# Four places instead of two for the output-gate tiles of the mLSTM in a hybrid block

## The chip, the cores and the metric

The kernel runs on one core of a Trainium2 chip. The core has five engines that run side by side, each through its own queue of instructions in order: PE (TensorE) for matmuls and transposes, DVE (VectorE), ACT (ScalarE) and POOL (GpSimd) for the work on elements, and SP (SyncE), which here issues nearly all DMAs. Data lies in DRAM, in the on-chip memory (SBUF, 128 partitions) and in PSUM, into which PE writes.

The metric is the time of one execution on the device in microseconds. Times inside an execution are counted from its first instruction. A trace is of one execution, recorded by the hardware profiler.

## The reference: what is computed

The input x is [1, 1024, 1024]. One layer projects its norm h with a wide matrix and runs two branches:

```python
qk = silu(conv(a_q, a_k));  mq, mk, mv = heads(...)          # 4 heads of width 256
h_fw = mlstm_one_direction(mq, mk, mv, i_fw, lf_fw)
h_bw = flip(mlstm_one_direction(flip(mq), flip(mk), flip(mv), flip(i_bw), flip(lf_bw)))
hm  = rmsnorm(h_fw + h_bw, ml_norm_g)
y_a = hm * sigmoid(a_o) * silu(a_z)                          # the output gate
y_b = rmsnorm(diff_attention(dq, dk, da_v, lam)) * silu(b_z) # 8 heads of width 128
mix = sigmoid(g_a + gb[0]) * (y_a @ w_branch_a) + sigmoid(g_b + gb[1]) * (y_b @ w_branch_b)
out = rmsnorm(x + mix @ w_out, final_g)
```

The change concerns the line of `y_a`. The product of the two functions of a_o and a_z is made early in the kernel and kept in DRAM; it is called the gate here.

## The kernel before, in words

**Precision.** Every float32 matrix product is made of three products of halves: a high part (names ending in H, cast by ACT) and a low part (names ending in L, a subtraction on DVE or POOL).

**Stages.** The kernel runs one stage after the other: the norm and the transposition of x; the products for a_k, a_q, a_o and a_z with the convolution, whose results go to DRAM (the gate to the eight tensors `gm`, 128 channels by 1024 positions each); the attention, head by head, whose results go to the eight tensors `yb`; the mLSTM (from about 1107 us to about 1398 us in the trace), whose results go to the eight tensors `ya`; and the output stage, which first multiplies `yb` with `w_branch_b`, then `ya` with `w_branch_a`, and then the mix with `w_out`. Products for the two mixing gates (`gate_units`: 48 matmuls into a PSUM tile `pj` per half, a tanh on ACT at L837 into a tile `gt`, a store at L838 into `tga` or `tgb`) are spread over all stages as filling for PE.

**The mLSTM.** Both directions of a head are computed together. Its 1024 positions are four chunks of 256, and each chunk is two steps of 128 positions, so a head has eight steps (t = 0 to 7 in `ml_units`, L1239). In a step PE makes the state's products (`I`), the product of the weights with the values (`P`), the scores of the next step (`S`) and transposes of the weights W (`T`); DVE turns the scores into W (L1139), the denominators into factors (L1165 to L1176), combines the two directions in W (L1185) and adds up the result `hm` (L1188, L1209); POOL masks W (L1136); ACT scales (L1179, L1183) and casts (L1198). A head's tail (norm, transposition, gate) runs during the first steps of the next head: the scaling by the norm (L1216) at t = 1 and 2, the output `O(0)` for the first 512 positions at t = 2 and `O(1)` for the other 512 at t = 3. The last head's tail is the list `late` (L1307), put ahead of the filling that follows.

**The gate tiles.** `load_g(half)` (L1218) loads two tiles `gA` of 128 channels by 512 positions (i = 0, 1) for one half of a head's positions. `out(i, half)` (L1223) transposes `hm` on PE into a PSUM tile `T`, multiplies it with the norm's gain and the gate tile on DVE (L1228), with the result in the same gate tile, and stores this tile to `ya` (L1229). In the written program `load_g(0)` of a head stands at t = 0 of the next head and `load_g(1)` at t = 2, behind `O(0)` (L1300); for the last head, `load_g(0)` stands at L1306 and `load_g(1)` behind `O(0)` in `late`. A head needs four gate tiles, and the tag `gA` has two places in SBUF.

**What sets the order.** PE's instructions run in the order in which the program writes them (`keep(E.PE)`, L1522). The order of all other queues is set at build by a planner: among the instructions that can go, it takes the one that is earliest in the program, and it counts a tile as free to be written once its place has no user left. A load can therefore go out long before its place in the program, but not before a place of its tag is free. On the chip each instruction waits for the semaphores of what it needs, and what stands behind it in its queue waits too.

**The pools.** SBUF is handed out in pools, one per stage: `w1` for the attention, `w2` for the mLSTM, `wy` and `wr` for the output stage. They use the same bytes one after the other (`reuse_waits="tile"`: a tile waits for the last user of its own bytes). `gA` is the last tag of `w2`. `w2` closes behind `late` and the filling beside it (L1574), then `wy` opens.

**The output stage's start.** `load_y` (L1310) loads one of the eight `yb` tensors into a tile `yraw` (L1312; two places), casts it on ACT into a tile `sl_yb` (L1314) and subtracts on DVE into another (L1315). The first matmul group of the stage goes through all eight in turn, with three matmuls each (L429). On ACT, L1314 stands among the tanh of the filling (L837) and the casts of the next weights (L204, into one of three places `wH`).

Of the kernel before, what the change touches and what calls it, by code (L numbers as in the profile page):

```python
# [7 lines left out]
F32 = mybir.dt.float32  # L8
# [101 lines left out]
class Block:  # L110
# [917 lines left out]
    def ml_head(self, n, st):  # L1028


        v, a, p, q, w2 = self.v, self.a, self.p, self.q, self.w2
# [185 lines left out]

        def load_g(half):  # L1218
            for i in range(2):
                st["g", i] = w2.tile([128, 512], F32, name="gA", tag="gA", bufs=2)  # L1220
                q.dma_start(out=st["g", i], in_=self.gd_ml[2 * n + i][:, half * 512:(half + 1) * 512])

        def out(i, half):  # L1223
            ps = self.bank("T")
            for k in range(4):
# [8 lines left out]
                    v=self.v_units("av", n, vv, order=(3, 2, 1, 0)), weigh=step(weigh),  # L1234
                    state=lambda c, d: [do(state, c, d, i) for i in range(2)], split=step(split), S=step(scores),
                    I=step(t_tile), T=step(transposes), P=step(pv), scale=step(scale), g=step(load_g),
                    O=lambda half: [do(out, i, half) for i in range(2)])

# [402 lines left out]
```

## Time and profile before

| What | Value |
|---|---|
| Median of 3 runs | 1697.88 us (1696.63 to 1701.5) |
| The profiled execution's own time | 1699.79 us |
| Its span, first to last instruction | 1698.0 us |
| Mean granted TensorE clock | 0.996 |
| Busy share of PE / DVE / ACT / POOL | 97% / 59% / 45% / 37% |
| Gate loads gA<-gm (L1221) | 16 of 256 KB, first at 1150.2 us, last at 1393.5 us |
| Multiplies with the gate (L1228) | 16 of 128x512, median 750 ns, first at 1224.0 us, last at 1397.0 us |
| Stores ya<-gA (L1229) | 16, first at 1224.7 us, last at 1397.8 us |

How to read the rows that follow. A row of a timeline has its start, its length, engine and line, operation, the tile written and the tiles read, their shapes, and in brackets the idle time of the engine just before it and what ended it. Engine names with a q (SPq) are instructions of the queue itself, such as the issue of a DMA; "x2" joins two in a row. A row of windows has a stretch's start and end, its length, the busy time and the count of instructions of PE, PE's weight loads, DVE, ACT and POOL, the granted clock of PE (1.00 is full speed), the share of the DMA engines' time and GB/s. Matmuls overlap, so the length of one is more than the time between two.

### The profile page before, as it was taken

Reading aid. Unit: us, or ns where it says so; the run is one execution under the profiler, and the core shown is the slowest. Engines: PE = TensorE matmul, PEld = TensorE weight load, DVE = VectorE, ACT = ScalarE, POOL = GpSimd, SP = SyncE. Lnnn points to the kernel's source line nnn. Section 1 sums busy time; section 2 is a strip of 40 time slices with the busy share of each in tenths; the row PEclk is TensorE's granted clock in tenths of the full one; section 3 lists DMA queues with packets and bytes.
Section 4 is the critical chain, followed back from the end, with each engine's and each line's share of the span. In section 5 each row is a group of like instructions: output and inputs, shape, how many; then the busy total and the mean of one; then the engine's idle time right before and its main releaser. Section 6 shows DMA issues by size and latency. Waiting matters only on the chain. (4 is left out here: it accounts for less than half of the span.)

```text
span 1698.0 us, 25367 instructions
## 1 busy us (share of the span) xinstructions
PE 1650.1 (97%) x9431; PEld 1387.7 (82%) x9431; DVE 994.1 (59%) x1799; ACT 760.0 (45%) x1522; POOL 635.3 (37%) x712
## 2 busy tenths in 40 slices
PE   7999999999999999999999999999999898999998
PEld 5777887887888988898888888889999777888887
DVE  5778668674277666766666765126666644135533
ACT  6454555543254454454445454325656644022221
POOL 5767676665343235424351431221331311212000
PEclk9999999999999999999999999999999999999999
DMA  5334434434231213221230221175554327344222
GB/s 179 101 118 134 137 115 134 124 124 137 75 81 44 63 38 87 63 63 37 76 88 26 63 75 63 50 208 155 143 170 140 104 93 244 119 142 136 87 92 83
DMA packets 175630, 178.79 MB, mean 105 GB/s; under 512 B 12185, under 2 KB 135410, under 8 KB 175506
## 3 DMA queue, kind: packets, MB, share of 16 engines
q1 hardware_dynamic: 174594, 175.58, 34.5%
q8 instruction: 74, 1.21, 0.3%
q10 hardware_dynamic: 912, 1.59, 0.2%
q14 instruction: 50, 0.41, 0.1%
HBM read 114.11 MB, written 46.24 MB: 94 GB/s over the span
## 5 line engine op out<-in xcount | busy, mean ns | idle before, releaser
L429 PE MATMUL pj<-hH,wH 128*128 128x512 f32 x640 | 266.3, 416 | 3.3 <-ACT f L542 1.5
L429 PE MATMUL pj<-hH,wL 128*128 128x512 f32 x640 | 251.9, 394 | 1.7 <-POOL wL L207 1.7
L429 PE MATMUL pj<-hL,wH 128*128 128x512 f32 x640 | 250.6, 392 | 0.2 <-DVE hL L580 0.2
L209 POOL TENSOR_TENSOR wL<-raw,wH 128x1024 fp32r<-128x1024 f32 x41 | 99.6, 2429 | 284.2 <-ACT wH L204 281.8
L928 ACT ACTIVATE e<-S,nm 128x1024 f32<-128x1024 f32 x128 | 142.7, 1115 | 134.2 <-DVE nm L926 133.9
L948 DVE TENSOR_TENSOR pL<-T,pH 128x512 fp32r<-128x512 f32 x128 | 87.9, 688 | 117.4 <-ACT pH L947 116.7
L926 DVE TENSOR_REDUCE nm<-S 128x1 f32<-128x1024 f32 x128 | 150.5, 1217 | 10.1 <-PE S L923 9.3
L429 PEld LDWEIGHTS pj<-hH,wH 128*128 128x128 f32 x640 | 120.7, 189 | 37.8 <-issue 14.4
L451 PE MATMUL pj<-wH,hH 128*128 128x256 f32 x512 | 149.9, 293 | 1.6 <-DVE vL L1035 1.3
L451 PE MATMUL pj<-wL,hH 128*128 128x256 f32 x512 | 144.9, 283 | 1.4 <-POOL wL L207 1.4
L429 PEld LDWEIGHTS pj<-hH,wL 128*128 128x128 f32 x640 | 120.4, 188 | 30.1 <-POOL wL L207 3.1
L451 PE MATMUL pj<-wH,hL 128*128 128x256 f32 x512 | 144.5, 282 | 0.0
L429 PEld LDWEIGHTS pj<-hL,wH 128*128 128x128 f32 x640 | 121.0, 189 | 18.2 <-DVE hL L580 0.6
L429 PE MATMUL pj<-sl_yb,wH 128*128 128x512 f32 x384 | 121.8, 397 | 4.7 <-ACT sl_yb L1314 2.1
L947 ACT CAST pH<-T 128x512 fp32r<-128x512 f32 x128 | 74.7, 584 | 100.5 <-PE T L131 99.9
L204 ACT CAST wH<-raw 128x1024 fp32r<-128x1024 f32 x56 | 58.8, 1050 | 126.8 <-PE pj L429 86.4
L923 PE MATMUL S<-kst,qq 64*128 64x512 f32 x768 | 106.5, 408 | 0.0
L451 PEld LDWEIGHTS pj<-wH,hH 128*128 128x128 f32 x512 | 97.7, 191 | 6.8 <-issue 3.9
L451 PEld LDWEIGHTS pj<-wL,hH 128*128 128x128 f32 x512 | 97.5, 190 | 2.3 <-POOL wL L207 2.3
L451 PEld LDWEIGHTS pj<-wH,hL 128*128 128x128 f32 x512 | 97.7, 191 | 0.1
L429 PEld LDWEIGHTS pj<-sl_yb,wH 128*128 128x128 f32 x384 | 73.3, 191 | 22.8 <-DVE sl_yb L1315 3.3
L934 DVE SCALAR_TENSOR_TENSOR e<-e,r,e 128x1024 f32<-128x1024 f32 x64 | 88.8, 1388 | 2.2
(358 smaller groups left out, 4099.9 us busy)
## 6 DMA issues: line engine op xcount, KB each, us to landing
raw<-in_w_in_dram SPq DMA_DIRECT2D x88, 512.0 KB, 3.8
kst<-hl SPq DMA_DIRECT2D x64, 128.0 KB, 2.4
qq<-hl SPq DMA_DIRECT2D x64, 128.0 KB, 2.4
x<-in_x_dram SPq DMA_DIRECT2D x8, 512.0 KB, 6.2
cak<-y SPq DMA_DIRECT2D x16, 256.0 KB, 2.3
cakH<-cin SPq DMA_DIRECT2D x16, 256.0 KB, 4.4
cakL<-tz SPq DMA_DIRECT2D x16, 256.0 KB, 4.0
gm<-oz SPq DMA_DIRECT2D x16, 256.0 KB, 2.8
```

What stands on the lines that cost most here:

```text
L204: self.a.copy(wH, raw)
L209: self.p.tensor_tensor(out=wL, in0=raw, in1=wHf, op=ALU.subtract)
L429: self.t.matmul(ps, lhsT=l[:, k, :], rhs=r, start=(n == 0), stop=(n == 23))
L451: self.t.matmul(ps[:, i, :], lhsT=l, rhs=r[:, k, :], start=(kh == 0 and k == 0 and m == 0), stop=(kh == 1 and k == 3 and m == 2))
L923: self.t.matmul(ps[:, o], lhsT=qq[r, x, c], rhs=k[r, y, o], start=(m == 0), stop=(m == 2))
L926: v.tensor_reduce(out=nm, in_=ps, axis=AX.X, op=ALU.max, negate=True)
L928: a.activation(out=e, in_=ps, func=AF.Exp, bias=nm[:, 0:1], accum_out=Z[:, j, t:t + 1])
L934: v.scalar_tensor_tensor(out=e0, in0=e, scalar=r[:, 0:1], in1=e0, op0=ALU.mult, op1=ALU.add)
L947: a.copy(pH[:, :, s], ps)
L948: v.tensor_tensor(out=pL[:, :, s], in0=ps, in1=pH[:, :, s].bitcast(F32), op=ALU.subtract)
```

## The change

The tag of the gate tiles gets four places in SBUF instead of two. Nothing else in the program is touched: the instructions, their number and PE's order are the same. Two more tiles of 2 KB a partition make the pool `w2` 4 KB larger; since the pool ends at a fixed address and `gA` is its last tag, the other tiles of the pool lie 4 KB lower.

```diff
         def load_g(half):
             for i in range(2):
-                st["g", i] = w2.tile([128, 512], F32, name="gA", tag="gA", bufs=2)
+                st["g", i] = w2.tile([128, 512], F32, name="gA", tag="gA", bufs=4)
                 q.dma_start(out=st["g", i], in_=self.gd_ml[2 * n + i][:, half * 512:(half + 1) * 512])
```

## The prediction

> **What bounds the kernel now.** I read the page first: TensorE is busy nearly all the time, so a change counts only where it shortens a wait of PE or a slow stretch of its clock.
>
> ```profile
> PE 1650.1 (97%) x9431; PEld 1387.7 (82%) x9431; DVE 994.1 (59%) x1799; ACT 760.0 (45%) x1522; POOL 635.3 (37%) x712
> ```
>
> Next I asked for the two lines that use the gate tiles (gA): their loads (L1221) and their multiplies (L1228), with what DVE waited for ahead of a multiply.
>
> ```profile
> L1221 SPq DMA_DIRECT2D gA<-gm x16: 319/320/531, 1150.2 to 1393.5; - x16
> DMA to landing us min/median/max: 3.1/3.9/5.2
> ...
> L1228 DVE SCALAR_TENSOR_TENSOR gA<-T,mlg,gA x16: 741/750/753, 1224.0 to 1397.0; 128x512 f32<-128x512 f32 x16
>   DMA gA<-gm: 7.0, 3
>   issue: 2.2, 1
> ```
>
> DVE waits for a gate tile ahead of four of the 16 multiplies: three are put down to the DMA, and the one put down to "issue" is of the same cause, as the timeline below shows. PE does not wait for a gate tile by name. The windows show where it stands (length, then PE busy; the number behind POOL is the granted clock):
>
> ```profile
> 1160.00:1200.00 40.00, 39.98 (x336) 39.70 (x335) 26.19 (x101) 22.63 (x56) 6.16 (x21) 1.00 0.40 108
> ...
> 1352.80:1357.40 4.60, 0.69 (x3) 0.14 (x1) 2.44 (x11) 0.88 (x2) 0.00 (x0) 0.99 0.39 116
> 1357.40:1360.80 3.40, 3.33 (x10) 2.76 (x11) 0.83 (x3) 1.17 (x3) 0.69 (x2) 0.51 0.61 189
> 1420.00:1430.70 10.70, 6.46 (x23) 4.12 (x23) 4.90 (x4) 5.54 (x7) 2.49 (x1) 0.92 0.78 225
> 1430.70:1435.80 5.10, 5.10 (x12) 4.05 (x13) 1.95 (x3) 2.09 (x2) 0.00 (x0) 0.50 0.54 169
> 1435.80:1512.00 76.20, 76.20 (x337) 63.07 (x337) 14.90 (x18) 10.81 (x11) 16.73 (x7) 1.00 0.39 124
> ```
>
> There are two holes, from 1353 and from 1420, and behind each a stretch at half clock. Behind the second PE is full for 76 us: what is gained ahead of it is kept.
>
> **Place A: the second half of head 2, during head 3.** The timelines of DVE, PE and SP:
>
> ```profile
> 1352.74 0.75 DVE L1228 SCALAR_TENSOR_TENSOR gA<-T,mlg,gA 128x512 f32<-128x512 f32 x1 [0.71 <-DMA gA<-gm]
> 1354.09 0.15 DVE L1176 TENSOR_TENSOR al<-rr,gc_sint 128x2 f32<-128x2 f32 x1
> 1356.40 0.75 DVE L1228 SCALAR_TENSOR_TENSOR gA<-T,mlg,gA 128x512 f32<-128x512 f32 x1 [2.15 <-issue]
> 1357.07 0.34 DVE L1185 SCALAR_TENSOR_TENSOR W<-W,rr,W 128x128 f32<-128x128 f32 x1
> ...
> 1354.44 0.33 PE L131 MATMUL T<-ident,W 128*128 128x128 f32 x1 [1.28 <-ACT W L1183]
> 1357.47 0.48 PE L131 MATMUL T<-ident,W 128*128 128x128 f32 x1 [2.70 <-DVE W L1185]
> ...
> 1348.74 0.38 SPq L1229 DMA_DIRECT2D ya<-gA  x1
> 1353.34 0.32 SPq L1221 DMA_DIRECT2D gA<-gm  x1
> ```
>
> With two places, a half's load can start only when the store of the half before has left the same place. SP holds the load until 1353.34, 4.6 us behind the store of 1348.74. It lands near 1356.4 (the shortest landing above, 3.1 us), and that is when the multiply starts. PE waits for the next head's W, which stands behind the multiply in DVE's queue. With four places this load needs no store of its own head: it goes out one half earlier. The store and the reload around 1353 stay, and so does SP's wait there, but the reload then carries head 3's first half, which is first used at 1388.53 (below).
>
> The sum for A: without the 0.71 and the 2.15, `al` ends at 1353.53 (1354.24 - 0.71), the multiply takes 0.67 of DVE's queue (1357.07 - 1356.40), and L1185 ends at 1354.54 (another 0.34) instead of 1357.41. PE resumes 2.9 us earlier. Of its waits 1.28 - 0.71 = 0.6 stays and about as much for L1185: the chain from rr by L1183 to L1185 is late next, not the load. Waits that short leave the clock alone; even one of 1.80 did, as the window behind it shows:
>
> ```profile
> 1333.18 0.44 PE L131 MATMUL T<-ident,W 128*128 128x128 f32 x2 [1.80 <-DVE W L1185]
> ...
> 1333.20:1340.00 6.80, 6.80 (x47) 6.17 (x48) 5.45 (x21) 6.48 (x18) 1.39 (x4) 1.00 0.12 36
> ```
>
> So the 3.3 us of busy PE at 0.51 shrink by half, 1.6 us. A gives 2.9 + 1.6 = 4.5 us; at the least 0 (the loads stay where they are), at the most 1.28 + 2.70 + 1.6 = 5.6.
>
> In sentences that the rest can do without: the Trainium skill (TensorE: Matmul & The Clock Gate, Part 1) says that the clock gate looks at free-running windows of some 3.4 us and passes half of the pulses behind an idle one, which gives an estimate of 1.7 us lost by one window. The trace's 3.40 us at 0.51 agree.
>
> **Heads 0 and 1** give nothing: the four waits for gA are the two of A and the two of B, and no other multiply waits.
>
> **Place B: the end of head 3 and the start of the output stage.**
>
> ```profile
> 1389.43 1.23 PE T L131 x8
> ...
> 1388.53 1.41 DVE L1228 SCALAR_TENSOR_TENSOR gA<-T,mlg,gA 128x512 f32<-128x512 f32 x2 [2.16 <-PE T L131]
> 1395.77 0.75 DVE L1228 SCALAR_TENSOR_TENSOR gA<-T,mlg,gA 128x512 f32<-128x512 f32 x1 [5.82 <-DMA gA<-gm]
> 1397.02 0.75 DVE L1228 SCALAR_TENSOR_TENSOR gA<-T,mlg,gA 128x512 f32<-128x512 f32 x1 [0.51 <-DMA gA<-gm]
> 1429.37 1.22 DVE L1315 TENSOR_TENSOR sl_yb<-yraw,sl_yb 128x1024 fp32r<-128x1024 f32 x1 [1.90 <-ACT sl_yb L1314]
> ...
> 1392.90 0.96 SPq L1221 DMA_DIRECT2D gA<-gm  x2
> 1393.96 0.38 SPq L838 DMA_DIRECT2D tga<-gt  x1
> 1396.54 1.58 SPq L1229 DMA_DIRECT2D ya<-gA  x2
> 1398.23 0.37 SPq L1312 DMA_DIRECT2D yraw<-yb  x1
> ...
> 1408.87 1.05 ACT L204 CAST wH<-raw 128x1024 fp32r<-128x1024 f32 x1 [2.95 <-PE pj L429]
> 1419.21 1.05 ACT L1314 CAST sl_yb<-yraw 128x1024 fp32r<-128x1024 f32 x1 [6.03 <-DMA yraw<-yb]
> ...
> 1419.55 0.39 PE L429 MATMUL pj<-hH,wL 128*128 128x512 f32 x1
> 1421.46 0.40 PE L429 MATMUL pj<-sl_yb,wL 128*128 128x512 f32 x1
> 1422.15 0.39 PE L429 MATMUL pj<-sl_yb,wL 128*128 128x512 f32 x1
> ```
>
> All times here are on the old scale, since A moves them together. The transposes are done by 1390.66, but the last two multiplies end only at 1397.77, and SP issues the output stage's first load (yraw) right behind their stores. With four places both gate loads have long landed and the multiplies end near 1391.6 (two of 0.75 behind 1389.94, a little later where a transpose is). Their stores go out by 1392, and the first yraw load between 1392 and 1394.4, in front of or behind the tga store of 1393.96: 6.2 to 3.8 us earlier.
>
> From there eight loads pass through two places, two at a time: a landing (median 4.5, row below), a cast (1.05) and a subtraction (1.22) are 6.8 us a pair and 27.1 for four, and the second subtraction adds 1.2. Counted from 1398.23 this ends at 1426.5; in fact it ended at 1430.6. 4.1 us were lost, the largest part that I can name at ACT's wH cast of 1408.87, which waits for PE while a yraw tile stands behind it.
>
> ```profile
> DMA to landing us min/median/max: 3.4/4.5/6.3
> L429 PE MATMUL pj<-sl_yb,wH 128*128 128x512 f32 x16 | 6.4, 462 | 4.3 <-ACT sl_yb L1314 2.1 <-DVE sl_yb L1315 1.2 <-ACT gt L837 1.0
> ```
>
> PE needs the eighth tile at 1419.8 + 7 x 0.69 = 1424.6 (0.69 us for the three matmuls of a tile, from 1421.46 to 1422.15). The chain's new end is 1394.4 + 28.3 = 1422.7 at best, or 1426.8 if the 4.1 are lost again. I take the late one, as the same queues serve the same loads. It leaves PE late by 2.2 of today's 4.3 us. A wait in pieces under 1.80 leaves the clock alone, so the 5.1 us at 0.50 shrink by 2.6. B gives 4.3 - 2.2 + 2.6 = 4.7; at the least 0 (the chain hangs on PE's release of wH, and all moves together), at the most 4.3 + 2.6 = 6.9.
>
> **What it adds.** Two more loads can go out near 1150: two SP issues of 0.5 us (0.96 for two) ahead of loads for head 1, hidden since PE stands full from 1160 to 1200, 39.98 of 40.00 us; without that cover 1 us. The pool w2 grows by 4 KB a partition, so its tiles lie elsewhere against those of the pools before and after, and each waits for the last reader of its bytes. SP's first load into w2 goes out at 1107.01, behind the last store of the pool before, and the tile that PE needs first from ACT is written 14 us later, so I cost this at nothing; uncovered it is some of those 14 us.
>
> ```profile
> 1107.01 0.92 SPq L1040 DMA_DIRECT2D akf<-cak  x2
> 1121.54 0.45 ACT L1081 ACTIVATE kwH<-T,gc_ws 128x256 fp32r<-128x256 f32 x1
> ```
>
> The number of instructions stays the same, and no wait is added. The sum, 4.5 + 4.7 = 9.2 us, is made on an execution of 1699.79 us (span 1698.0, 1.79 around it). That is 1.9 above the median of the runs, 1697.88, from which I take the sum off: 1688.7.
>
> **The rivals.** *A alone.* The yraw casts keep their order on ACT behind the wH casts that PE releases, and B moves with PE: 1697.88 - 4.5 = 1693.4. For it: 2.95 us of ACT's wait at 1408.87 end with PE. Against: ACT's order is set at build by when loads are expected, and these come earlier.
>
> *The clock is not the waits' doing.* Then only the waits go: 1697.88 - 2.9 - 2.1 = 1692.9. Against it, both slow stretches begin at a hole. The Trainium skill (TensorE: Matmul & The Clock Gate, the practical table) asks only that no idle gap exceed about 3 us, by which the 2.70 would not slow the clock; the trace has the half clock right behind it.
>
> *No change.* The planner issues the loads no earlier than now: 1697.9. For it: they stand late in the program. Against: head 0's first load went out at 1150.2 for a multiply at 1224.0, as soon as a place was there.
>
> *Slower.* In B the casts stand in front of the tanh that frees PE's bank (gt) while their loads land late: ACT's 6.03 us at 1419.21 held gt back, and PE lost 1.0. If four halves lost 1.0 each and each cost a slow stretch like A's 1.6, that is 10.4 more, less A's 4.5: 1703.8. It decides once ACT's head waits over 5.5 us (24 matmuls of 0.23, a half) beyond a half's end; the longest landing is 6.3.
>
> **How the numbers follow.** Chances: forecast 0.54, A alone 0.20, clock 0.07, no change 0.11, slower 0.08. The likeliest is 1688.7, with a range of its own from 1697.88 - 5.6 - 6.9 = 1685.4 to 1692.8. The range of all reaches over "A alone" with half of A lost, to 1695.7, and leaves out no change and slower. A measurement here can tell about 0.3%, 5.1 us, from no change, so faster means under 1692.8: 0.53 of the forecast, 0.05 of A alone, 0.03 of the clock, 0.61. Slower is 0.08 and 0.01 of no change, and the same is the rest, 0.30.
>
> **What would show it.** A: in head 3 the multiplies of head 2's second half start with no wait for gA, PE's wait of 2.70 falls to about 0.6, and the clock stays at 1.00 there. B: no gate load behind 1360, the last multiply ends within 2 us of the transposes, the first yraw load starts within 4 us of them, and PE's waits for sl_yb fall to about 2 us. Wrong would be: waits of DVE for gA that stay; A's gain with B's waits as long as before; a longer wait of PE for gt.

## The result and the profile after

The changed kernel took 1688.2 us in the median of six runs (1687.29 to 1690.33), beside 1698.73 for the kernel before (1696.63 to 1701.5, six runs): a ratio of 0.9935 with a 95% interval from 0.9925 to 0.9945, or 10.5 us. In a second comparison, of five runs, it was 1689.49 beside 1698.96, ratio 0.9946 [0.9932, 0.9961], or 9.5 us. The profiled execution took 1687.36 us, its span 1685.6.

The first page of the profile of after, the line of the engines, and what the trace says of the gate's loads and multiplies (the loads' landing time under the loads):

```profile
PE 1645.8 (98%) x9431; PEld 1385.3 (82%) x9431; DVE 992.4 (59%) x1799; ACT 760.3 (45%) x1522; POOL 635.2 (38%) x712
...
L1221 SPq DMA_DIRECT2D gA<-gm x16: 319/320/737, 1148.4 to 1356.1; - x16
DMA to landing us min/median/max: 2.8/5.1/5.4
...
L1228 DVE SCALAR_TENSOR_TENSOR gA<-T,mlg,gA x16: 740/746/751, 1222.2 to 1384.5; 128x512 f32<-128x512 f32 x16
  PE T L131: 2.4, 2
```

No multiply waits for a gate load any more: what is left in front of them is 2.4 us of waiting for transposes. The loads land more slowly than before (5.1 us in the median against 3.9), and that costs nothing, as each is now early: the last one goes out at 1356.1 for the multiply that starts at 1384.5.

PE runs the same 9431 matmuls in the same order, so the two traces can be laid side by side, matmul by matmul. The lead of after over before is 0.5 us or less up to the mLSTM. It then grows in three steps and shrinks in one: 1.8 at the mLSTM's entrance, 6.3 behind place A, 14.7 behind place B, and 12.4 from 1432 to the end.

**Place A.** Timelines of after (DVE, SP, PE), and its windows there:

```profile
1351.65 0.74 DVE L1228 SCALAR_TENSOR_TENSOR gA<-T,mlg,gA 128x512 f32<-128x512 f32 x1
1352.31 0.34 DVE L1185 SCALAR_TENSOR_TENSOR W<-W,rr,W 128x128 f32<-128x128 f32 x1
...
1351.75 0.32 SPq L1221 DMA_DIRECT2D gA<-gm  x1
...
1351.92 0.33 PE L131 MATMUL T<-ident,W 128*128 128x128 f32 x1 [0.47 <-ACT W L1183]
1352.70 0.33 PE L131 MATMUL T<-ident,W 128*128 128x128 f32 x1 [0.45 <-DVE W L1185]
...
1352.42:1355.84 3.42, 3.14 (x21) 2.88 (x22) 1.05 (x3) 1.07 (x3) 0.69 (x2) 1.00 0.70 230
```

The multiplies start without a wait, L1185 ends at 1352.65 and PE's waits of 1.28 and 2.70 are 0.47 and 0.45. The reload still stands in SP's queue at 1351.75, but what it carries is used 30 us later. The clock stays at 1.00. The lead grows by 4.55 us, from 1.71 just ahead of place A to 6.26 behind it: 3.05 at the two waits and 1.5 over the ten matmuls that ran at half clock before.

**Place B.** Timelines of DVE, SP, ACT and PE of after:

```profile
1382.25 1.41 DVE L1228 SCALAR_TENSOR_TENSOR gA<-T,mlg,gA 128x512 f32<-128x512 f32 x2 [2.16 <-PE T L131]
1383.86 1.41 DVE L1228 SCALAR_TENSOR_TENSOR gA<-T,mlg,gA 128x512 f32<-128x512 f32 x2 [0.19 <-PE T L131]
1416.79 1.22 DVE L1315 TENSOR_TENSOR sl_yb<-yraw,sl_yb 128x1024 fp32r<-128x1024 f32 x1 [0.64 <-ACT sl_yb L1314]
1424.26 1.23 DVE L1315 TENSOR_TENSOR sl_r<-yraw,sl_r 128x1024 fp32r<-128x1024 f32 x1 [2.38 <-ACT sl_r L1314]
1425.40 0.68 DVE L1339 SCALAR_TENSOR_TENSOR sl_mb<-tgl,pj 128x512 f32<-128x512 f32 x1
...
1383.03 2.58 SPq L1229 DMA_DIRECT2D ya<-gA  x4
1387.69 0.86 SPq L1312 DMA_DIRECT2D yraw<-yb  x2
...
1403.25 1.05 ACT L204 CAST wH<-raw 128x1024 fp32r<-128x1024 f32 x1
...
1418.25 0.61 PE L429 MATMUL pj<-sl_yb,wH 128*128 128x512 f32 x2
1426.14 0.50 PE L429 MATMUL pj<-sl_yb,wH 128*128 128x512 f32 x1 [1.61 <-DVE sl_mb L1339]
...
1409.00:1424.00 15.00, 15.00 (x68) 12.43 (x67) 4.90 (x4) 6.96 (x8) 2.49 (x1) 1.00 0.80 234
```

All four multiplies of the last head follow its transposes and end at 1385.27. The eighth `yb` tile is ready at 1418.01 (1416.79 + 1.22), and PE takes it at 1418.25, just in time: in the window from 1409 PE is full and its clock at 1.00, where before there stood 4.3 us of waits and 6.8 us at half clock. That is a lead of 8.4 us. Then comes a wait that the kernel before did not have: 1.61 us at 1426.14 for the first gated sum (L1339), which frees PE's bank. In DVE's order it stands behind two subtractions (L1315) of the `ya` tiles, of which the second waits for its cast; before, it stood ahead of them. At 1431.99 PE is held up a second time for the same reason. The lead shrinks by 1.9 us behind the first and by 0.4 behind the second: 2.3 us are given back.

**The entrance.** The first wait of PE in the mLSTM, before and after:

```profile
1122.13 0.36 PE L127 MATMUL T<-vH,kwH 128*128 128x258 f32 x1 [1.68 <-ACT kwH L1081]
```

```profile
1120.35 0.36 PE L127 MATMUL T<-vH,kwH 128*128 128x258 f32 x1 [0.15 <-ACT kwH L1081]
```

These 1.5 us lie 28 us ahead of the first gate load, and no step of the prediction has them.

### The profile page after: what moved, and what is told of

It is laid out like the page before. It is cut to its first block, busy times and chain, and to the rows that moved or that the text cites. A ratio compares the mean times of both kernels' runs of the same rounds, so it can differ in the third digit from the quotient of the medians.

```text
span 1685.6 us, 25370 instructions
## 1 busy us (share of the span) xinstructions
PE 1645.8 (98%) x9431; PEld 1385.3 (82%) x9431; DVE 992.4 (59%) x1799; ACT 760.3 (45%) x1522; POOL 635.2 (38%) x712
## 3 DMA queue, kind: packets, MB, share of 16 engines
q10 hardware_dynamic: 912, 1.59, 0.2%
## 5 line engine op out<-in xcount | busy, mean ns | idle before, releaser
L204 ACT CAST wH<-raw 128x1024 fp32r<-128x1024 f32 x56 | 58.8, 1050 | 114.7 <-PE pj L429 75.8
L923 PEld LDWEIGHTS S<-kst,qq 64*128 64x128 f32 x768 | 67.8, 184 | 26.2 <-issue 10.5
```

The costliest lines, as they stand in the source:

```text
L204: self.a.copy(wH, raw)
L923: self.t.matmul(ps[:, o], lhsT=qq[r, x, c], rhs=k[r, y, o], start=(m == 0), stop=(m == 2))
```

## Experiments

Each kernel's time stands beside runs of the kernel before on the same chip. Idle operations in these kernels are a maximum of a tile with itself, and all kernels compute the whole of the reference.

**Two places of double width: the layout alone.**

```diff
-                st["g", i] = w2.tile([128, 512], F32, name="gA", tag="gA", bufs=2)
+                st["g", i] = w2.tile([128, 1024], F32, name="gA", tag="gA", bufs=2)[:, 0:512]
```

> The kernel before with two places as before, but each place twice as wide (128x1024, of which the first 512 columns are used), so that the tiles behind it lie at the same addresses as with four places. Theory (the four places act only through the waits that they remove): the time stays that of the kernel before, 1697 to 1700 us, the 1.28 and 2.70 us holes of TensorE and its half clock at head 2's second half stay, and the first weight loads of the output stage stay where they were. Rival (the layout of the pool moves something by itself, such as the 1.5 us that the changed kernel gained at the entrance of the mLSTM, where no output gate is in flight yet): 1.5 us below the kernel before, and the 1.68 us wait at the entrance is short.

Measured: 1700.76 us beside 1699.90, ratio 1.0006 [0.9995, 1.0016]. The holes are there, here 1.65 and 3.54 us, and the half clock too. So the 4 KB that `w2` grows by, and the shift of its tiles, move nothing; the gain is the places'. At the entrance the first wait is 0.89 us, and the layout is not what shortens it.

**Only head 2's second half has its own places.**

```diff
-                st["g", i] = w2.tile([128, 512], F32, name="gA", tag="gA", bufs=2)
+                st["g", i] = w2.tile([128, 512], F32, name=(o := "gB" if (n, half) == (2, 1) else "gA"), tag=o, bufs=2)
```

> Only head 2's second half has its own two tiles; all other halves, head 3's too, share the old two. Theory (the two places of gain are independent): 4.4 us below the kernel before, 1694.3; TensorE's two holes at head 2's second half become 0.4 to 0.5 us each and the half clock there is gone, while the loads of yraw at the start of the output stage come as late after the matmuls around them as before, with the gaps and the half clock there. Rival of the forecast (the half clock belongs to the place and not to the holes): 1.6 us less gain, 1696, with the half clock still in the profile.

Measured: 1695.08 us beside 1699.90, 4.8 less, ratio 0.9970 [0.9958, 0.9981]. PE's second wait at place A (the first is 0.47 us) and DVE's second multiply of the second half at place B, in this kernel:

```profile
1354.70 0.33 PE L131 MATMUL T<-ident,W 128*128 128x128 f32 x1 [0.45 <-DVE W L1185]
...
1393.09 0.75 DVE L1228 SCALAR_TENSOR_TENSOR gA<-T,mlg,gA 128x512 f32<-128x512 f32 x1 [0.88 <-DMA gA<-gm]
```

Place A is as in the changed kernel and place B as before: 4.5 us of waits for `gt` and `sl_yb`, and 6.8 us at half clock. The size is that of the forecast's term A, and PE's lead over before grows by 4.5 us at place A in this trace too.

**Only head 3's second half has its own places** (the same edit with `(3, 1)`).

> Only head 3's second half has its own two tiles. Theory: the holes and the half clock at head 2's second half stay, and the start of the output stage gains what it gained in the changed kernel, 8.4 us less the 2.0 given back at the wait for the first sl_mb: 6.4 us below the kernel before, 1692.3. By the forecast's sum it would be 4.7 us, 1694.0. Rival (the second place only gains because the first has moved the work ahead of it): under 3 us, 1696 or more.

Measured: 1692.39 us beside 1699.90, 7.5 less, ratio 0.9953 [0.9938, 0.9967]. PE's second wait at place A, and the last multiplies, the first `yraw` load and the eighth subtraction at place B:

```profile
1355.96 0.33 PE L131 MATMUL T<-ident,W 128*128 128x128 f32 x1 [2.57 <-DVE W L1185]
...
1387.08 1.41 DVE L1228 SCALAR_TENSOR_TENSOR gA<-T,mlg,gA 128x512 f32<-128x512 f32 x2 [2.16 <-PE T L131]
1392.52 0.86 SPq L1312 DMA_DIRECT2D yraw<-yb  x2
1421.39 1.23 DVE L1315 TENSOR_TENSOR sl_yb<-yraw,sl_yb 128x1024 fp32r<-128x1024 f32 x1 [0.53 <-ACT sl_yb L1314]
```

A is as before, with its half clock, and B has no wait and full clock; the wait for L1339 is there with 1.35 us. Place B's gain needs nothing of A's. At 7.5 us it is nearer to the expectation's 6.4 than to the forecast's 4.7. In this kernel's trace the lead grows by 8.4 us at place B and 2.4 are given back at L1339. The two halves alone make 12.3 us where both together measured 9.5 and 10.5, which their intervals (some 2 us each way) allow.

**Three places** (`bufs=3`).

> Three places. Theory: the first gate of a second half finds a free place and the second has to wait for the first store of the half before it. At head 2 that is still early enough for most of the gain there (about 3 to 4.4 us of 4.35), at the end of head 3 the second gate is asked for behind one store only, so that the last two multiplies end some 2 to 4 us earlier than before instead of 12: between 1690.5 and 1695 us. Rival (only the count of places, all four, frees the queue): no gain, 1698.

Measured: 1693.22 us beside 1699.90, 6.7 less, ratio 0.9957 [0.9941, 0.9974]. In this kernel, the last multiply and PE's longest wait at place B:

```profile
1390.63 0.75 DVE L1228 SCALAR_TENSOR_TENSOR gA<-T,mlg,gA 128x512 f32<-128x512 f32 x1 [5.08 <-DMA gA<-gm]
1421.61 0.80 PE L429 MATMUL pj<-sl_yb,wH 128*128 128x512 f32 x1 [1.60 <-DVE sl_yb L1315]
```

A is gained whole (0.48 and 0.46 us). At B one gate load still waits for a store, the last multiply for that load, and 3.0 us of waits with 6.8 us at half clock are left. The fourth place is worth what is missing to the changed kernel: its 9.5 and 10.5 us are 2.8 and 3.8 more than these 6.7.

**The last store of head 3 held up, with four places.**

```diff
-            v.scalar_tensor_tensor(out=g, in0=ps, ..., in1=g, op0=ALU.mult, op1=ALU.mult)
+            v.scalar_tensor_tensor(out=g, in0=ps, ..., in1=g, op0=ALU.mult, op1=ALU.mult); [v.tensor_tensor(out=g, in0=g, in1=g, op=ALU.max) for _ in range(9 if (n, half, i) == (3, 1, 1) else 0)]
             q.dma_start(out=self.ya[2 * n + i][:, half * 512:(half + 1) * 512], in_=g)
```

> The changed kernel, and behind head 3's last gate multiply nine idle VectorE operations on the gate's tile (a maximum with itself, 5 to 6 us in all) ahead of its store. Theory (the gain at the start of the output stage is that the last multiply and store no longer hold the queue of the yraw loads and the casts behind them): yraw's loads come 5 to 6 us later than in the changed kernel, the waits for sl_yb and the half clock come back in part, and the time is 3 to 7 us above the changed kernel, 1691 to 1695. Rival (the gain there is only that TensorE comes through head 3 sooner): 1688, as the changed kernel.

Measured: 1697.69 us beside 1699.33, ratio 0.9993 [0.9984, 1.0002]: the gain is gone, since place B loses what place A gains. That is more than expected, 8.2 us above the changed kernel's 1689.49 and not 3 to 7. In this kernel (DVE, SP, PE, windows):

```profile
1385.89 6.51 DVE L1228 TENSOR_TENSOR gA<-gA 128x512 f32<-128x512 f32 x9
1427.66 1.23 DVE L1315 TENSOR_TENSOR sl_yb<-yraw,sl_yb 128x1024 fp32r<-128x1024 f32 x1 [4.29 <-ACT sl_yb L1314]
1396.70 1.77 SPq L1312 DMA_DIRECT2D yraw<-yb  x2
1427.68 0.80 PE L429 MATMUL pj<-sl_yb,wH 128*128 128x512 f32 x1 [3.04 <-ACT sl_yb L1314]
...
1417.67:1421.08 3.41, 1.25 (x4) 0.50 (x4) 2.21 (x2) 1.65 (x3) 2.26 (x1) 1.00 0.48 156
1421.08:1424.49 3.41, 2.94 (x5) 1.27 (x5) 1.23 (x1) 1.03 (x1) 0.00 (x0) 0.50 0.93 242
...
1427.91:1431.32 3.41, 2.95 (x7) 1.96 (x8) 2.10 (x3) 1.04 (x1) 0.00 (x0) 0.50 0.36 115
```

Place A is as in the changed kernel (0.46 and 0.46 us). At place B there are 6.6 us of waits for `sl_yb` and 13.7 us at half clock, twice the kernel before's (four windows of 3.41 us, of which two are shown behind the one that set them off). The half clock costs some 4.8 us, an estimate: half of the 9.7 us that PE was busy in the four windows. The idle operations do not hold up the subtractions by themselves, since DVE stands idle for 10.45 us ahead of the first one, at 1402.86. What they hold up is SP's queue: the last store goes out at 1392.43, and the first `yraw` load stands behind it. So the start of the `yraw` loads sets the waits at B, and the clock adds to their price. The 6.5 us of idle operations made that load 8.5 us later than in the changed kernel (13.9 against 5.4 in the table below), later than in the kernel before too. In this kernel the planner has put a gate store (1393.96) and a weight load (1395.90) between the two, so how much is the store's alone is not shown.

The four kernels at place B, in time since head 3's first multiply (from the rows of each kernel, those of before in the prediction: 1398.23 - 1388.53 = 9.7, 1430.59 - 1388.53 = 42.1, and so on):

| Kernel | First yraw load | Eighth subtraction ends | Between them | PE waits for gt, sl_yb | Half clock |
|---|---|---|---|---|---|
| before | 9.7 | 42.1 | 32.4 | 4.3 | 6.8 |
| after | 5.4 | 35.8 | 30.3 | none over 0.3 | none |
| only head 3 | 5.4 | 35.5 | 30.1 | none over 0.3 | none |
| last store late (first multiply at 1382.85) | 13.9 | 46.0 | 32.2 | 6.6 | 13.7 |

The chain of the eight tiles is about 2 us shorter where the load is early. It shows first at the fifth load, which starts 13.0 us behind the first in after (1400.68) and 15.3 before (1413.57). What goes with it is ACT's order: the planner has put casts of `sl_yb` ahead of casts of `wH` (L204) there, and the `wH` cast at 1403.25 no longer waits for PE with a landed tile behind it, as the one at 1408.87 did before for 2.95 us. The order by itself was not tried, and the loads of L1312 also land sooner in after (4.0 us in the median against 4.5), so that the order is the cause is argued and not shown.

**Holes of chosen length at place A, with four places.** Two, three and eight idle operations.

```diff
-            dg = slice(b * 128, (b + 1) * 128)
+            dg = slice(b * 128, (b + 1) * 128); [v.tensor_tensor(out=Wc, in0=Wc, in1=Wc, op=ALU.max) for _ in range(3 if (n, tt) == (3, 3) else 0)]
             v.scalar_tensor_tensor(out=Wc[:, dg], in0=Ws[1 - dw][:, dg], ...
```

> The changed kernel, and in head 3's step 3 three idle VectorE operations (a maximum of Wc with itself, which changes nothing) ahead of the one at line 1185 for which TensorE's transposes wait. Theory (the half clock at head 2's second half came of the holes' length): the hole of 0.45 us becomes about 1.4 us, TensorE's clock stays full, and the work behind it comes 0.5 to 1.0 us later. Rival (any hole there halves the clock): half clock as in the kernel before, 1.6 us more.

> As the run with three idle operations, but with eight, some 2.7 us. Theory (length decides): the hole becomes 2.5 to 3.1 us, TensorE's records show half clock for some 3.4 us behind it, and the work behind it comes 2.7 us of hole and 1.6 us of half clock later, 4.3 in all. Rival (the clock belongs to something else than the hole): full clock and only 2.7 us later.

Measured in one execution each: 1691.4 us with three and 1694.0 with eight. An idle operation takes 0.42 to 0.45 us, and the two holes run into one. PE's wait and the window behind it, first with three and then with eight:

```profile
1354.66 0.77 PE L131 MATMUL T<-ident,W 128*128 128x128 f32 x2 [2.61 <-DVE W L1184]
...
1354.33:1357.74 3.41, 3.08 (x8) 2.44 (x9) 0.96 (x3) 1.15 (x3) 0.69 (x2) 0.50 0.64 226
```

```profile
1357.46 0.77 PE L131 MATMUL T<-ident,W 128*128 128x128 f32 x2 [4.89 <-DVE W L1184]
...
1357.27:1360.68 3.41, 3.22 (x9) 2.53 (x10) 0.82 (x3) 1.15 (x3) 0.69 (x2) 0.50 0.50 159
```

Three gave a hole of 2.61 us, not the 1.4 that the expectation was made for, and half clock. So the clock follows the hole, with the load's wait gone, and the rival "the clock is not the waits' doing" falls. But a hole of 4.89 us bought no more half clock than one of 2.61: 3.41 us in both. That led to the next run.

> The changed kernel with two idle VectorE operations (a maximum of Wc with itself) ahead of line 1185 in head 3's step 3: a hole of about 2.2 us. Theory (the clock is decided in fixed windows of 3.413 us, whose place against the kernel differs from run to run: a window in which TensorE stood idle for 1.86 us or more is followed by one at half clock, and one with 1.82 us or less is not): half clock if 1.86 us of the hole lie in one window of the grid that the half-clock record at the end of the run gives away, full clock if the grid cuts the hole so that both parts are shorter. Rival (the length of one hole decides, with a bound between 1.80 and 2.61 us): the same whatever the place of the grid. By either, the work behind it comes 1.3 us of hole later than in the changed kernel, and up to 1.7 us more with the half clock.

Measured in one execution: 1690.2 us. Its hole is 2.13 us. Two windows of this kernel at place A:

```profile
1350.51:1353.93 3.42, 1.48 (x10) 1.00 (x9) 3.42 (x14) 1.38 (x4) 0.00 (x0) 1.00 0.30 99
1353.93:1357.34 3.41, 3.21 (x9) 2.52 (x10) 0.83 (x3) 1.15 (x3) 0.69 (x2) 0.50 0.65 236
```

The grid put 1.94 us of idle PE (3.42 - 1.48) into one window, and half clock followed, as the windows' rule had it. The grid did not cut the hole, so this run does not by itself set the rule against a bound on the length of one hole. Other traces do, under "What was not expected": a hole of 1.95 us that the grid cut was followed by full clock, and shorter ones within one window by half clock.

**The subtractions of the ya tiles on GpSimd: the 2.3 us that are given back.**

```diff
-        self.v.tensor_tensor(out=l, in0=raw, in1=h.bitcast(F32), op=ALU.subtract)
+        (self.p if src is self.ya else self.v).tensor_tensor(out=l, in0=raw, in1=h.bitcast(F32), op=ALU.subtract)
```

> The changed kernel with the eight subtractions behind the ya loads of line 1315 on GpSimd instead of VectorE, so that the first gated sum (line 1339, sl_mb) does not stand behind them on VectorE. Theory (the 1.61 us wait of TensorE for that sum at 1426.14 and the 0.41 us one after it are the 2.0 us that the changed kernel gives back): both waits go, and the time is 1.5 to 2.0 us below the changed kernel, 1686.3. Rival (GpSimd, which also makes the low parts of the weights there, becomes late, and TensorE waits for wL): no gain, or 1 to 5 us above the changed kernel.

Measured: 1691.29 us beside 1699.33, ratio 0.9952 [0.9939, 0.9966]. Against the changed kernel's 1689.49 of the next comparison this version neither gained nor lost much. The waits for L1339 are gone, as the theory had it. The rival's waits for wL did not come. Two others stand where the last four subtractions were moved (each 2.4 us on GpSimd, 1.2 on VectorE). They are 1.46 and 1.48 us long in the trace, not the 1.10 and 1.31 that the next expectation gives. The first of them:

```profile
1507.32 0.50 PE L429 MATMUL pj<-sl_yb,wH 128*128 128x512 f32 x1 [1.46 <-POOL sl_yb L1315]
```

**Only the first four on GpSimd** (`src is self.ya and i < 4`), beside the changed kernel once more.

> The changed kernel, and only the four subtractions behind the first four ya loads (sl_r, line 1315) on GpSimd; the last four stay on VectorE. Theory: TensorE's waits of 1.61 and 0.41 us at the first gated sums go, as they went with all eight moved, and the waits of 1.10 and 1.31 us near 1507, which stood where the last four had been moved, do not come: 2.0 to 2.3 us below the changed kernel of the same comparison. Rival (GpSimd's subtractions hold up the weights' low parts): TensorE waits for wL and nothing is gained.

> The changed kernel once more, unaltered, beside the version below. Theory: 10.5 us below the kernel before, as in the first comparison; the wait of TensorE at the mLSTM's entrance, 1.68 us in the profile of before and 0.15 in the first of after, comes out anywhere between the 0.4 and 1.7 us that the other kernels' profiles showed there, since nothing that the change touches sets it. Rival (the change itself shortens that wait): 0.15 us again.

Measured: 1686.12 us (1685.81 to 1688.92), ratio to before 0.9929 [0.9916, 0.9941]; the changed kernel 1689.49 (1689.17 to 1690.42). GpSimd's four subtractions, and PE from the first gated sum on, in this version; then the same window of the first profile of after:

```profile
L1315 POOL TENSOR_TENSOR sl_r<-yraw,sl_r x4: 2389/2398/2402, 1422.3 to 1432.8; 128x1024 fp32r<-128x1024 f32 x4
...
1425.00:1500.00 75.00, 75.00 (x332) 62.14 (x331) 11.29 (x16) 11.99 (x12) 23.89 (x10) 1.00 0.42 130
```

```profile
1425.00:1500.00 75.00, 73.74 (x324) 60.76 (x325) 13.89 (x19) 11.31 (x11) 16.79 (x7) 1.00 0.39 123
```

Both waits are gone and no new one has come. Beside the second profile of after, where these two were 0.86 and 0.32 us, the version gains 1.8 us there; beside the first profile it gains 2.3. The medians are 3.4 us apart, and the ranges of the runs do not touch in this comparison; the rest of the difference lies at the entrance and in the clock's windows, which differ from run to run. So this version is probably the fastest of those measured; 1.8 to 2.3 us of the 3.4 are explained.

The rerun of after had 0.52 us at the first wait of the entrance, inside what was expected, and a second wait of 1.83 us at 1146.66 with half clock behind it. Over all profiles the first wait was 0.15 to 0.65 us in the eight profiles of kernels with four places and 0.88 to 1.68 in the five of kernels with fewer places of one tag, which I did not expect. The second wait stands the other way, so the sum of both is 1.5 to 2.5 us with four places and 1.2 to 3.0 with fewer. Nothing is gained there on the whole, so I leave the 1.5 us of the first pair of profiles out of the change's account; that they are chance is argued, not shown. The first wait by itself is shorter with four places in every profile, with the layout of `w2` ruled out (0.89 us with the wide tiles), and why is open.

## Why the prediction was right, step by step

1688.7 us was forecast, and 1688.2 and 1689.49 were measured. The sum came out near its mark because errors went against each other, which is luck: place B was worth 3.7 us more than forecast, and 2.3 us were given back that no step had. The median that the sum was taken from, 1697.88 of three runs, also lay 0.85 us below that of six.

- **Place A, 4.5 us.** Right, with its mechanism: 4.55 us on PE in the traces, 4.8 in the run that changes only this place. The waits gave 3.05 against 2.9, the half clock 1.5 against 1.6. PE's waits of 0.47 and 0.45 are those worked out (0.6 and about as much). The reload stayed in SP's queue, as said.
- **Heads 0 and 1, nothing.** Right: between 1122 and 1350 the lead moves by less than 0.1 us.
- **Place B, start of the chain.** Right: the last multiply ends 0.9 us behind the transposes (1384.37 to 1385.27), and the first `yraw` load, at 1387.69 and so 1393.97 on the old scale (plus the lead there, 1388.53 - 1382.25 = 6.28), lies between 1392 and 1394.4, behind the tga store.
- **Place B, end of the chain: the step that failed.** I took the late end, 1426.8, "if the 4.1 are lost again". It was 1424.29 (1418.01 + 6.28): about half of the 4.1 us were lost again. PE needs the tile at 1424.6, and so it waits not 2.2 us but not at all. My reason for the late end, that the same queues serve the same loads, left out that the order of ACT's queue is planned anew when the loads come earlier; under the rival "A alone" I had that very argument. That the order made up those 2 us is likely, but not shown by itself.
- **Place B, the clock.** The half clock was 6.8 us, from 1429.01, and not the 5.1 from 1430.7 that I read off a window that I had cut myself. All of it went, worth some 3.0 us (half of the 6.0 that PE was busy in it) and not 2.6. With the 4.3 us of waits that is 7.3 of the lead of 8.4; the rest goes with the slower first matmuls behind the waits (0.49 to 0.80 us against 0.39). B was 8.4 us where I had 4.7.
- **"A wait in pieces under 1.80 leaves the clock alone."** Wrong as a rule. In the run with three places pieces of 0.48 and 1.60 us were followed by half clock.
- **What it adds.** The earlier issues cost nothing, as said: no new wait of PE behind 1148. "No wait is added" was wrong of the planned order. L1339 fell behind two subtractions on DVE, which gave back 2.3 us (1.8 in the second profile). No rival had that. The layout of `w2` costs nothing, as said, and the run with wide tiles shows it.
- **The rivals.** "A alone" falls with the run that changes only head 3. "The clock is not the waits' doing" falls with the chosen holes. "No change" falls with the loads' times. "Slower" by tanh behind casts: PE's wait for `gt`, 1.0 us before, is gone.

On PE's trace the sum is then 4.55 + 8.4 - 2.3 = 10.65 us for the change, against 9.2 forecast; the rest of that pair's 12.4 us is the 1.5 at the entrance and small differences ahead of it.

## What to carry to other kernels

A buffer count is worth what stands in the queue behind the load it holds back: here four of sixteen loads mattered, those of two half heads, because of an L1185 and a first `yraw` load that stood behind what they held up. When a stall goes, look at the order in which the queues are then planned, for the gain (casts ahead of `wH`) and for what falls behind (L1339) alike. And count TensorE's idle time together with its neighbours: waits that are harmless one by one (1.61 us at L1339 in after, 0.47 at place A) are followed by half clock when they fall close together (0.48 and 1.60 us in the run with three places).

## What was not expected of the hardware

The half clock comes in fixed windows. Its records in a trace lie on a grid of 3.413 us that is another in each execution: in the profile of before they begin at 1357.33 and 1429.01, which is 21 times 3.413 apart. With TensorE at full clock, a window in which it was idle for 1.83 us or more (the least such: after's second profile, below) was, from 30 us on, followed by one at half clock in all thirteen profiles, and one with 1.82 us or less by full clock, but for two. (Ahead of 30 us, where PE transposes x, four more windows with 1.58 to 1.70 us idle were followed by half clock.) Rows of the kernel with three places, of the second profile of after, and of one of the two exceptions (the version with four subtractions on GpSimd):

```profile
1329.16:1332.57 3.41, 1.59 (x9) 1.01 (x8) 1.79 (x11) 1.27 (x4) 2.56 (x4) 1.00 0.40 105
1332.57:1335.98 3.41, 3.41 (x27) 3.09 (x26) 2.21 (x10) 3.24 (x9) 0.53 (x2) 1.00 0.19 54
1417.90:1421.32 3.42, 1.55 (x5) 0.48 (x3) 2.18 (x2) 1.55 (x3) 2.46 (x1) 1.00 0.53 134
1421.32:1424.73 3.41, 2.21 (x4) 0.98 (x5) 1.46 (x2) 1.04 (x1) 0.00 (x0) 0.50 0.91 294
```

```profile
1144.27:1147.68 3.41, 1.58 (x11) 1.19 (x10) 0.69 (x1) 2.04 (x3) 2.31 (x6) 1.00 0.83 189
1147.68:1151.10 3.42, 3.42 (x19) 3.42 (x18) 0.00 (x0) 0.00 (x0) 1.05 (x3) 0.50 0.81 233
```

```profile
1380.15:1383.57 3.42, 2.19 (x13) 1.33 (x12) 1.31 (x2) 3.29 (x8) 1.57 (x4) 1.00 0.11 34
1383.57:1386.98 3.41, 3.41 (x12) 2.85 (x12) 1.60 (x3) 0.00 (x0) 0.00 (x0) 0.50 1.05 364
```

Of a row, the first number behind the length is PE's busy time and the 1.00 or 0.50 the granted clock: 1.55 and 1.58 us of work are followed by 0.50, 1.59 by 1.00. In the exceptions 2.19 and 2.04 us of work (idle 1.23 and 1.37) were followed by 0.50 as well; there PE ran transposes and short matmuls, and what the gate counts is perhaps not what the records show as busy. A window at half clock is left only with more work: 2.95 us were followed by half clock again (the late-store kernel at 1427.91), 3.21 by full.

The idle times in a window are added up, whether in one hole or in several. The length of one hole alone does not decide. In the second profile of after, the hole of 1.83 us at the mLSTM's entrance lies within one window, and half clock follows. In the run with three idle operations the hole there is longer, 1.95 us, but the grid (62 windows ahead of the record at 1354.33) cuts it at 1146.11, and the clock stays full:

```profile
1146.51 0.35 PE L451 MATMUL pj<-wH,hH 128*128 128x256 f32 x1 [1.95 <-DVE vL L1035]
...
1142.70:1146.11 3.41, 1.86 (x9) 1.20 (x7) 0.44 (x1) 2.08 (x3) 0.90 (x3) 1.00 0.91 217
1146.11:1149.53 3.42, 3.02 (x25) 3.06 (x26) 0.25 (x1) 0.04 (x1) 2.48 (x6) 1.00 0.79 253
```

The Trainium skill (TensorE: Matmul & The Clock Gate, Part 1) gives the same free-running window of 3413 ns, and the traces agree. The Trainium skill (TensorE: Matmul & The Clock Gate, Part 1) also advises to avoid idle gaps over about 3.4 us; here 1.83 us within one window were enough, and the measurement decides. Since the grid lies differently in each execution, nearly the same hole costs a half window or none, as these two show. That fits runs of one kernel that lie 2 to 3 us apart, but this was not tried by itself.
